# Hybrid decoder layer: the memory branch's output product as seven quarter products, with the weight sums made in DRAM

## The chip, the core and the metric

The kernel runs on one core of one Trainium2 chip. Its time is the device time of one execution, in microseconds; the time before is the median of three runs. The profile is of one further execution. TensorE (PE in the views) multiplies, VectorE (DVE) and ScalarE (ACT) work on tiles in SBUF and PSUM, GpSimd (POOL) and SyncE (SP) mostly issue DMAs.

## What is computed

One decoder layer on 512 tokens of 1024 features. Three token mixers run side by side: a sliding-window attention (branch 0), a stick-breaking attention (branch 1) and a cross-attention to 256 memory rows (branch 2). Each gives 512 features per token, is multiplied by its branch weights (512 x 1024), gated, and summed. Then follow an output product, normalisation with residual, and a SwiGLU feed-forward part.

```python
g = jax.nn.sigmoid(gl.reshape(B, S, N_BRANCH, D))
merged = (g[:, :, 0] * jnp.einsum('bse,ed->bsd', y_swa, w_branch_swa[l])
          + g[:, :, 1] * jnp.einsum('bse,ed->bsd', y_sb, w_branch_sb[l])
          + g[:, :, 2] * jnp.einsum('bse,ed->bsd', y_mem, w_branch_mem[l]))
mix = jnp.einsum('bsd,de->bse', merged, w_out[l])
h = h + rms_norm(mix, ln_mix_post[l])
```

## The kernel before

**Split products.** Float32 factors are split into a high part (rounded, made by ScalarE) and a low part (the rest, made by VectorE). `mm3` makes a product as three TensorE products: high by high, high by low, low by high. So each weight tile of 128x1024 costs a load (SP), a high part (`hi`, ScalarE) and a low part (`lo`, VectorE) before TensorE can use it. `split` and `w_split` do this; all of them are recorded under line 202, so tiles tell them apart.

**The stream.** The work of TensorE up to the output product is a list of units in `dn`: projections, values, memory keys and values, gates, branch products. `Stream.piece` starts a unit by loading weights four units ahead, splitting three ahead, calling the unit's `begin` functions, and then issuing its products. Attention heads are issued in between. This fixes only the program order. The order in which each engine runs its instructions is written out by hand in ORDER, one list of program numbers for each engine, and PLAN gives each tile its buffer.

**The start.** [...] SP and ScalarE's queue load x (eight pieces x[0] to x[7] of 128x512, `xT`) and the first three weight tiles in pieces. Each x[k] is multiplied by its gain and split into `uh` and `ul`; TensorE then runs nine products for each k (three weight tiles by three). It has nothing else to do until all eight pieces are used. POOL first clears eight tiles (`qbl`), and later writes the row of norms to DRAM (`row_x`) and reads it back turned, for the scaling of the values.

**Quarter products.** The gates of all branches and the product of branch 0 are made as seven products of quarters instead of eight. Tokens are cut into two halves and features into two halves; the factors are sums of quarters. For the gates and for branch 0 the sums of weight quarters were made by DMAs that add into the raw weight buffer in place, issued by POOL one after the other as the previous use of the buffer ended (`q_issue`, `seven_issue`). The sums of y are made on VectorE (`seven_sums`, four operations), after ScalarE has copied y in quarters (`seven_raw`), and split by `seven_split`. `seven` issues 12 products for each of p1, p2, p5, p3, p6, p7, p4; `seven_end` copies p1 and p5 aside, joins results, and `seven_out` multiplies by the gate and adds.

**The memory branch and the mix.** The memory branch was made plainly by `branch_t`: two halves of the output, four token tiles each, four chunks of y, three products. After each tile VectorE multiplies by the gate and adds the sum of the others. `merge(0)` turned (transposed on TensorE) the left half of the merged features for all four token tiles, `merge(1)` the right half, each followed by a split; `mix_mm` multiplies the turned tiles by the output weights `wo`, whose 16 tiles are split on ScalarE and VectorE during the gates and branch of the memory. The mix of tiles 0 and 1 was made in two halves, with `merge(1)` between them. Then `mix` normalises a tile of tokens and the feed-forward part begins.

Of the kernel before, what the change touches and what calls it, by code (L numbers as in the profile page):

```python
# [17 lines left out]
P = 128  # L18
# [3 lines left out]
KC = D // P  # L22
# [8 lines left out]
SEVENS = (SWA,)  # L31
# [19 lines left out]
    ),  # L51
    "vector": (
# [32 lines left out]
    ),  # L85
    "scalar": (
# [26 lines left out]
    ),  # L113
    "gpsimd": (
        "5-12 4 2-3 16 0 29 1 14 13 15 30 22 17 27 23 25 24 26 21 20 19 18 28 31-34 36-37 35 38 40 39 41-49 51 50 "
        "52-55 57 56 58-60 63 61-62 64-69 74 70 73 75 71-72 76-99 111-116 107 100-106 108-110"
    ),
    "sync": (
# [1928 lines left out]
```

## Time and profile before

| | us |
|---|---|
| median of 3 runs | 783.73 (783.63 to 783.98) |
| profiled execution | 783.61 |
| its span | 781.8 |
| TensorE busy in it | 773.5 |
| VectorE busy | 614.6 |
| ScalarE busy | 480.7 |
| POOL busy | 92.2 |

The span runs from the first instruction to the last; what lies around it is the difference to the execution's time. Matmuls overlap in the records, so a record is longer than the distance from one start to the next. Times in the views are us from the start of the span. The granted clock of TensorE was 0.999 of full speed.

### The profile page before, as it was taken

To read this page: it belongs to the slowest core of one execution; us is meant where nothing else is said; L and a number is where in the kernel's file an instruction comes from. 1 tells how busy PE (TensorE), PEld (TensorE's weight loads), DVE (VectorE), ACT (ScalarE), POOL (GpSimd) and SP (SyncE) were. 2 spreads that over 40 slices of the span, in tenths; PEclk is the share of its full clock that TensorE was granted. 3 is DMA by queue.
4 is the path that set the end of the run, shared out by engine and by line. 5 is a ranking of instruction groups with operands and counts; after the bars stand their busy time and mean duration, and the time that the engine had idled before them with its cause. 6 is when DMAs were issued, how large, how long until landed. Compare 5 with 4: busy or idle time off the path is not lost.

```text
span 781.8 us, 12301 instructions
## 1 busy us (share of the span) xinstructions
PE 773.5 (99%) x4626; PEld 678.8 (87%) x4626; DVE 614.6 (79%) x982; ACT 480.7 (61%) x862; POOL 92.2 (12%) x121
## 2 busy tenths in 40 slices
PE   9999999999999999999999999999999999999996
PEld 6899888788888888877888899999999999888885
DVE  6994787677887757999874599977777879997686
ACT  7662677786586658676653486445555456866662
POOL 3100400000112121020012001000000000215000
PEclk9999999999999999999999999999999999999999
DMA  8443923245459697589998138977767653959602
GB/s 302 141 130 122 319 84 109 81 135 149 94 122 199 164 193 168 98 225 205 338 334 169 22 82 232 252 190 189 186 178 189 176 160 99 232 113 246 123 2 107
DMA packets 44652, 130.18 MB, mean 167 GB/s; under 512 B 5296, under 2 KB 6880, under 8 KB 44592
## 3 DMA queue, kind: packets, MB, share of 16 engines
q1 hardware_dynamic: 30336, 84.68, 32.9%
q0 software_dynamic: 13824, 44.32, 30.1%
q8 instruction: 36, 0.59, 0.3%
q10 hardware_dynamic: 432, 0.39, 0.1%
q14 instruction: 24, 0.20, 0.1%
HBM read 122.55 MB, written 4.72 MB: 163 GB/s over the span
## 4 chain that ended last, share of the span: by engine, by line
PE 97%; DVE 1%; issue 0%; ACT 0%; DVEq 0%
PE p L202 97%; DVE lo L202 0%; DVE gq0p L202 0%; DVE gq2p L202 0%; ACT hi L202 0%; DVE fg L202 0%; DVE wo03l L202 0%; DVEq L2035 0%; DVE wo11l L202 0%; DVE wo02l L202 0%; DVE s L202 0%; DVE wide L202 0%; DVE wo00l L202 0%; ACT sqr L202 0%; DVE wo01l L202 0%
## 5 line engine op out<-in xcount | busy, mean ns | idle before, releaser
L202 DVE TENSOR_TENSOR lo<-raw,hi 128x1024 fp32r<-128x1024 f32 (+4 forms) x138 | 157.9, 1152 | 53.4 <-ACT hi L202 52.8
L202 ACT CAST hi<-raw 128x1024 fp32r<-128x1024 f32 (+4 forms) x138 | 136.3, 997 | 86.5 <-PE p L202 49.5
L202 ACT CAST hi<-wide 128x1024 fp32r<-128x1024 f32 x57 | 59.7, 1052 | 38.8 <-PE p L202 15.6
L202 DVE TENSOR_TENSOR lo<-wide,hi 128x1024 fp32r<-128x1024 f32 x57 | 69.7, 1224 | 17.2 <-ACT hi L202 16.9
L202 PE MATMUL p<-lo,lh 128*128 128x512 f32 x154 | 59.9, 389 | 0.0
L202 PE MATMUL p<-hi,ll 128*128 128x512 f32 x154 | 59.7, 389 | 0.0
L202 PE MATMUL p<-hi,lh 128*128 128x512 f32 x154 | 59.1, 389 | 0.0
L202 PE MATMUL p<-lo,uh 128*128 128x512 f32 (+1 forms) x160 | 57.3, 358 | 0.0
L202 PE MATMUL p<-hi,ul 128*128 128x512 f32 (+1 forms) x160 | 57.2, 358 | 0.0
L202 PE MATMUL p<-hi,uh 128*128 128x512 f32 (+1 forms) x160 | 56.2, 359 | 0.0
L202 PE MATMUL p<-uh,hi 128*128 128x512 f32 x136 | 54.5, 401 | 0.0
L202 PE MATMUL p<-uh,lo 128*128 128x512 f32 x136 | 53.0, 390 | 0.0
L202 PE MATMUL p<-ul,hi 128*128 128x512 f32 x136 | 53.0, 391 | 0.0
L202 POOL DMA_DIRECT2D wide<-in_w_gu x21 | 18.1, 877 | 185.7 <-DMA wide<-in_w_gu 150.9
L202 PEld LDWEIGHTS p<-lo,lh 128*128 128x128 f32 x154 | 28.9, 188 | 6.0
L202 PEld LDWEIGHTS p<-hi,ll 128*128 128x128 f32 x154 | 28.9, 188 | 6.0
L202 PEld LDWEIGHTS p<-hi,lh 128*128 128x128 f32 x154 | 28.9, 188 | 5.9
L202 PEld LDWEIGHTS p<-hi,uh 128*128 128x128 f32 x160 | 30.0, 188 | 4.3 <-DVE wide L202 0.3
L202 PEld LDWEIGHTS p<-lo,uh 128*128 128x128 f32 x160 | 30.0, 188 | 4.0 <-DVE lo L202 0.4
L202 PEld LDWEIGHTS p<-hi,ul 128*128 128x128 f32 x160 | 30.0, 188 | 3.7
L202 POOL DMA_DIRECT2D raw<-in_w_g x24 | 20.7, 861 | 104.8 <-DVE lo L202 95.4
L202 ACT COPY gp<-p 128x512 f32<-128x512 f32 x33 | 19.3, 586 | 22.0 <-PE p L202 21.4
(687 smaller groups left out, 2405.5 us busy)
## 6 DMA issues: line engine op xcount, KB each, us to landing
wide<-in_w_gu SPq DMA_DIRECT2D x31, 512.0 KB, 5.3
raw<-in_w_gu SPq DMA_DIRECT2D x26, 512.0 KB, 5.2
raw<-in_w_g POOLq DMA_DIRECT2D x24, 512.0 KB, 7.4
wide<-in_w_gu POOLq DMA_DIRECT2D x21, 512.0 KB, 8.4
raw<-in_w_g SPq DMA_DIRECT2D x18, 512.0 KB, 5.0
raw<-in_w_p SPq DMA_DIRECT2D x14, 512.0 KB, 3.7
raw<-in_w_brt SPq DMA_DIRECT2D x11, 512.0 KB, 4.8
bp<-in_w_dn SPq DMA_DIRECT2D x22, 256.0 KB, 6.4
```

Of the source, the lines that this page charges most:

```text
L202: ins = f(*args, **kw)
```

## The change

Branch 2 joins branch 0 in the seven quarter products. It takes the sums of weight quarters, for both branches, out of the raw buffers: for each of the two branches `w_sum` makes p5, p6, p4 and p7's weights in DRAM, by a copy and an adding DMA each, both on POOL, begun at units 17 to 24 in program order. p6's copy reads p5's sum, p4's reads p6's. The quarters are then loaded like any other weight. y of the memory branch is copied in quarters, and its four sums are made once the last pair of heads is out. `merge(i)` now turns both halves of the features for two token tiles: `merge(0)` tiles 0 and 1, `merge(1)` tiles 2 and 3. The mix of tile 0 and of tile 1 is each made in one go, and `merge(1)` follows them. All orders and buffer plans are written anew; the first entries of POOL's are shown.

```diff
-SEVENS = (SWA,)
+SEVENS = (SWA, MEM,)
+SUM_FROM = 17
...
     "gpsimd": (
-        "5-12 4 2-3 16 0 29 1 14 13 15 30 22 17 27 23 25 24 26 21 20 19 18 28 31-34 36-37 35 38 40 39 41-49 51 50 "
+        "5-12 31 33 4 39 41 32 34 40 42 16 2-3 35 0 43 29 36 1 44 37 45 38 14 13 15 30 46 17 22 27 21 20 19 18 23 "
...
-    def seven_issue(b, p):
-        j, h = QSRC[p]
-        src = a["w_brt"][:, b, h, 2 * j : 2 * j + 2].rearrange("p k n -> p (k n)")
-        if p in ("p1", "p2", "p3"):
-            sw[(b, p)] = w_load(src, 1024)
-            return
-        old = {"p5": "p1", "p6": "p5", "p4": "p6", "p7": "p3"}[p]
-        t = sw[(b, p)] = sw.pop((b, old))
-        nc.gpsimd.dma_start(t[:, :], src, accum_op=ALU.add)
+    wsum = {}
+    WSUM = dict(p5=((0, 0), (0, 1)), p6=("p5", (1, 1)), p4=("p6", (1, 0)), p7=((1, 1), (0, 1)))
+
+    def w_quarter(b, j, h):
+        return a["w_brt"][:, b, h, 2 * j : 2 * j + 2].rearrange("p k n -> p (k n)")
+
+    def w_sum(b, p):
+
+        old, more = WSUM[p]
+        t = wsum[(b, p)] = drm.tile([P, 1024], F32, name=f"ws{b}{p}")
+        nc.gpsimd.dma_start(t[:, :], wsum[(b, old)][:, :] if isinstance(old, str) else w_quarter(b, *old))
+        nc.gpsimd.dma_start(t[:, :], w_quarter(b, *more), accum_op=ALU.add)
...
+        return lambda: w_load(wsum[(b, p)][:, :] if p in WSUM else w_quarter(b, *QSRC[p]), 1024)
...
-    def merge(h):
+    def merge(i):
+
 
         for c in range(4):
-            pt = (dps if (h, c) in ((1, 0), (1, 1)) else aps)(f"mg{h}{c}")
-            for t in range(NT):
-                nc.tensor.transpose(
-                    pt[:, t * P : (t + 1) * P], gate_t[(MEM, t, h)][:, c * P : (c + 1) * P], ident[:, :]
-                )
...
+            pt = aps(f"mg{i}{c}")
+            for k in range(2):
+                h, o = divmod(2 * c + k, 4)
+                for t in range(2):
+                    nc.tensor.transpose(
+                        pt[:, (2 * k + t) * P : (2 * k + t + 1) * P],
+                        gate_t[(MEM, 2 * i + t, h)][:, o * P : (o + 1) * P],
+                        ident[:, :],
+                    )
...
-        for g, p in enumerate(QUART):
-            if p not in ("p1", "p2", "p3"):
-                dn.units[g0 + g - 5]["begin"].append(lambda p=p: seven_issue(b, p))
-        dn.units[g0 - 4]["begin"].append(lambda: seven_sums(b))
...
+        for i, p in enumerate(("p5", "p7", "p6", "p4")):
+            dn.units[SUM_FROM + 4 * SEVENS.index(b) + i]["begin"].append(lambda p=p: w_sum(b, p))
+        if b == SWA:
+            dn.units[g0 - 4]["begin"].append(lambda: seven_sums(b))
...
         if b in SEVENS:
             seven_raw(b, c, ps)
+            if b != SWA and c == 3:
+                seven_sums(b)
...
-    mix_mm(0, 0, 4)
+    merge(0)
+    mix_mm(0, 0, KC)
+    tmp[0] = mix(0)
+    mix_mm(1, 0, KC)
     merge(1)
-    mix_mm(1, 0, 4)
-    mix_mm(0, 4, KC)
-    tmp[0] = mix(0)
-    mix_mm(1, 4, KC)
```

POOL's numbers 31 to 46 in the new order are the 16 DMAs of `w_sum`, in pairs of copy and adding DMA: branch 0's p5, p7, p6, p4 (31 to 38), then branch 2's (39 to 46). 0 is the write of `row_x`, 1 its read-back, 5 to 12 the eight clears. In the new TensorE order the products of one x[k] with the three first weight tiles begin with the three high by high ones. In the new VectorE order the low parts of the output weights 05, 06, 07 and 14 to 17, and the last joins, multiplications and additions of token tiles 2 and 3, stand behind the low parts of `merge(0)`.

More of the change, by code (lines that the diff above doesn't have):

```diff
@@ L36 @@
     "tensor": (
[14 rows of a table removed]
[17 rows of a table added]
     ),
     "vector": (
[32 rows of a table removed]
[33 rows of a table added]
     ),
     "scalar": (
[26 rows of a table removed]
[28 rows of a table added]
     ),
     "gpsimd": (
-        "5-12 4 2-3 16 0 29 1 14 13 15 30 22 17 27 23 25 24 26 21 20 19 18 28 31-34 36-37 35 38 40 39 41-49 51 50 "
-        "52-55 57 56 58-60 63 61-62 64-69 74 70 73 75 71-72 76-99 111-116 107 100-106 108-110"
+        "5-12 31 33 4 39 41 32 34 40 42 16 2-3 35 0 43 29 36 1 44 37 45 38 14 13 15 30 46 17 22 27 21 20 19 18 23 "
+        "28 25 24 26 47-48 50 49 53 52 51 54-55 57 56 58-65 67 66 68-81 86 82 85 87 83-84 88-111 123-128 119 "
+        "112-118 120-122"
     ),
     "sync": (
-        "0-14 16-18 15 19-27 32 28-31 33-34 36-38 35 39-52 57 60 53-56 63-64 58-59 61-62 65-90 93-94 91-92 97-98 "
-        "95-96 99-211"
+        "0-14 16-18 15 19-27 32 28-31 33-34 36-38 35 39-52 57 60 53-56 63-64 58-59 61-62 65-94 97-98 95-96 101-102 "
+        "99-100 105-106 103-104 109 107-108 110-218"
     ),
@@ L124 @@
     "raw": (
-        "0 3 2 1 0 3 2 1 0 3 2 1 0 3 2 1 0 3 2 1 0 3 2 1 0 3 2 1 0 3 2 1 0 3 2 1 0 3 2 3 2 3 2 1 0 1 0 1 0 3 2 0 3 "
-        "1 3 1 3 1 2 3"
+        "0 3 2 1 0 3 2 1 0 3 2 1 0 3 2 1 0 3 2 1 0 3 2 1 0 3 2 1 0 3 2 1 0 3 2 1 0 3 2 3 2 3 2 1 0 1 0 1 0 3 1 2 0 "
+        "3 1 2 0 3 0 3 0 3 1 2 0 3 1"
     ),
@@ L129 @@
         "0 3 2 1 0 3 2 1 0 3 2 1 0 3 2 1 0 3 2 1 0 3 2 1 0 3 2 1 0 3 2 1 0 3 2 1 0 3 2 1 0 3 2 1 0 3 2 1 0 3 2 1 0 "
-        "3 2 1 0 3 2 1 0 3 2 1 0 3 2 1 0 3 2 1 0 3 2 1 0 3 2 1 0 3 2 1 0 3 2 1"
+        "3 2 1 0 3 2 1 0 3 2 1 0 3 2 1 0 3 2 1 0 3 2 1 0 3 2 1 0 3 2 1 0 3 2 1 0 3 2"
     ),
@@ L133 @@
         "0 3 2 1 0 3 2 1 0 3 2 1 0 3 2 1 0 3 2 1 0 3 2 1 0 3 2 1 0 3 2 1 0 3 2 1 0 3 2 1 0 3 2 1 0 3 2 1 0 3 2 1 0 "
-        "3 2 1 0 3 2 1 0 3 2 1 0 3 2 1 0 3 2 1 0 3 2 1 0 3 2 1 0 3 2 1 0 3 2 1"
+        "3 2 1 0 3 2 1 0 3 2 1 0 3 2 1 0 3 2 1 0 3 2 1 0 3 2 1 0 3 2 1 0 3 2 1 0 3 2"
     ),
     "p": (
[5 rows of a table removed]
[5 rows of a table added]
     ),
@@ L166 @@
         "0 14 15 13 1 12 2 4 3 5 7 6 8 10 9 11 15 0 14 12 13 1 3 2 4 5 6 7 8 9 10 11 0 1 15 13 14 12 2 4 3 5 6 11 "
-        "7 10 8 9 15 13 0 14 12 5 1 4 2 3 7 10 6 8 9 14 11 13 15 0 1 4 12 2 3 5 7 10 6 11 8 9 13 0 15 14 1 12 4 2 "
+        "7 10 8 9 15 13 0 14 12 5 2 4 1 3 7 10 6 8 9 14 11 13 15 0 2 4 12 1 3 5 7 10 6 11 8 9 13 0 15 14 2 12 4 1 "
         "6 11 3 8"
@@ L170 @@
     "spare": (
-        "0 3 1 2"
+        "1 4 2 3 4 0 1 3"
     ),
     "fraw": (
-        "0 8 7 6 5 1 2 4 3 0 8 7 6 5 0 1 3 4 6 7 2 0 8 5 1 4 7 3 6 2 8 1 0 5 4 3 2 7 6 8 0 4 1 5 3 7 8 2 6 0 1 3 4 "
-        "5 7 2 0 8 6 1 4 7 3"
+        "0 8 7 6 5 1 2 4 3 0 8 7 6 5 0 1 3 4 6 2 7 0 8 5 1 4 2 3 6 7 8 1 0 5 4 3 7 2 6 8 0 4 1 5 3 2 8 7 6 0 1 3 4 "
+        "5 2 7 0 8 6 1 4 2 3"
     ),
@@ L673, in mem_vals @@
         return gen
-    merged = [None] * 8
+    merged = {}
     QUART = ("p1", "p2", "p5", "p3", "p6", "p7", "p4")
@@ L827, in tile_kernel @@
     yq, ysum = {}, {}
-    def seven_issue(b, p):
-        j, h = QSRC[p]
-        src = a["w_brt"][:, b, h, 2 * j : 2 * j + 2].rearrange("p k n -> p (k n)")
-        if p in ("p1", "p2", "p3"):
-            sw[(b, p)] = w_load(src, 1024)
-            return
-        old = {"p5": "p1", "p6": "p5", "p4": "p6", "p7": "p3"}[p]
-        t = sw[(b, p)] = sw.pop((b, old))
-        nc.gpsimd.dma_start(t[:, :], src, accum_op=ALU.add)
-    def seven_got(b, p):
-        def got():
-            if p in ("p1", "p2", "p3"):
-                seven_issue(b, p)
-            return sw[(b, p)]
-        return got
+    wsum = {}
[7 more added lines that the diff above has]
+        nc.gpsimd.dma_start(t[:, :], w_quarter(b, *more), accum_op=ALU.add)
+    def seven_got(b, p):
+        return lambda: w_load(wsum[(b, p)][:, :] if p in WSUM else w_quarter(b, *QSRC[p]), 1024)
     def seven_raw(b, c, ps):
@@ L873, in seven_out @@
     def seven_out(b, t, h, x):
+        if b == SB:
+            acc_t[(t, h)] = x
+            return
         g = gate_t[(b, t, h)]
@@ L888, in seven_end @@
         if p in ("p1", "p5"):
-            t = spare(f"s{p}{b}{i}")
+            t = (ck if b == SB else spare)(f"s{p}{b}{i}")
             with tc.high_priority():
@@ L893, in seven_end @@
         elif p == "p2":
+            if b == SB:
+                t = ck(f"bs{i}")
+                nc.scalar.copy(t[:, :], ps[:, :])
+                ps = t
             seven_out(b, i, 0, ps)
@@ L908, in seven_end @@
             seven_out(b, 2 + i, 0, join(t, ps, t, ALU.add))
-            if b == MEM and i == 1:
-                merge(0)
     def seven(b, p):
@@ L957, in branch_t @@
         return gen
-    def merge(h):
+    def merge(i):
         for c in range(4):
-            pt = (dps if (h, c) in ((1, 0), (1, 1)) else aps)(f"mg{h}{c}")
-            for t in range(NT):
-                nc.tensor.transpose(
-                    pt[:, t * P : (t + 1) * P], gate_t[(MEM, t, h)][:, c * P : (c + 1) * P], ident[:, :]
-                )
-            mh, ml = ck(f"mgh{h}{c}", F32R), ck(f"mgl{h}{c}", F32R)
-            split(pt[:, :], mh[:, :], ml[:, :])
-            merged[4 * h + c] = (mh, ml)
+            pt = aps(f"mg{i}{c}")
[7 more added lines that the diff above has]
+                    )
+            merged[(i, c)] = ck(f"mgh{i}{c}", F32R), ck(f"mgl{i}{c}", F32R)
+            split(pt[:, :], merged[(i, c)][0][:, :], merged[(i, c)][1][:, :])
     for c in range(8):
@@ L985, in add_sevens @@
             dn.add(seven_got(b, p), 1024, seven(b, p))
-        for g, p in enumerate(QUART):
-            if p not in ("p1", "p2", "p3"):
-                dn.units[g0 + g - 5]["begin"].append(lambda p=p: seven_issue(b, p))
-        dn.units[g0 - 4]["begin"].append(lambda: seven_sums(b))
-        for g, p in ((1, "p5"), (2, "p3"), (3, "p6"), (4, "p7")):
-            dn.units[g0 + g]["begin"].append(lambda p=p: seven_split(b, p))
+        for i, p in enumerate(("p5", "p7", "p6", "p4")):
+            dn.units[SUM_FROM + 4 * SEVENS.index(b) + i]["begin"].append(lambda p=p: w_sum(b, p))
+        if b == SWA:
+            dn.units[g0 - 4]["begin"].append(lambda: seven_sums(b))
+        for g, p in ((2, "p5"), (3, "p3"), (4, "p6"), (5, "p7")):
+            dn.units[g0 + g - (b == SWA)]["begin"].append(lambda p=p: seven_split(b, p))
         dn.mark(f"branch{b}")
@@ L1462, in mix_mm @@
     def mix_mm(t, k0, k1):
-        tok = slice(t * P, (t + 1) * P)
-        if k0 == 0:
+        begun = t in mixed
+        if not begun:
             mixed[t] = [aps(f"mx{t}{h}") for h in range(2)]
-        order = [(h, k) for h in range(2) for k in range(k0, k1)] if k0 == 0 else [(h, k) for k in range(k0, k1) for h in range(2)]
+        order = [(h, k) for h in range(2) for k in range(k0, k1)] if not begun else [(h, k) for k in range(k0, k1) for h in range(2)]
         for h, k in order:
-            x = (merged[k][0][:, tok], merged[k][1][:, tok])
+            x = cols(merged[(t // 2, k // 2)], (k % 2) * 256 + (t % 2) * P, P)
             mm3(mixed[t][h][:, :], x, cols(wo[(h, k)], 0, 512), k == 0, k == KC - 1)
```

196 rows, old and new, of tables (ORDER, PLAN) are left out of this document.

## Prediction, before the result was known

> **What bounds the kernel now.** I read the page first: the span, the busy table, the chain that ended last.
>
> ```profile
> span 781.8 us, 12301 instructions
> PE 773.5 (99%) x4626; PEld 678.8 (87%) x4626; DVE 614.6 (79%) x982; ACT 480.7 (61%) x862; POOL 92.2 (12%) x121
> PE 97%; DVE 1%; issue 0%; ACT 0%; DVEq 0%
> ```
>
> TensorE is busy 99% of the span and is 97% of the chain. So a product less on TensorE is time saved, if nothing else makes TensorE wait. Next the pace of one product, from the timeline of the memory branch: the same factor pair on one token tile and on the next one, 12 products on.
>
> ```profile
> 380.12 0.39 PE L202 MATMUL p<-hi,y21l 128*128 128x512 f32 x1
> ...
> 382.84 0.39 PE L202 MATMUL p<-hi,y21l 128*128 128x512 f32 x1
> ```
>
> A record lasts 0.39 us, but 12 products start within 2.72 us, so one costs 0.227 us. Last the chain in order of time, for where something other than TensorE sets it, and the busy times of that stretch (columns: window, length, then busy us and count of PE, PEld, DVE, ACT, POOL; clock, DMA share, GB/s).
>
> ```profile
> 332.10 16.13 PE p L202 x71
> ...
> 349.35 1.17 DVE lo L202
> ...
> 358.84 1.23 DVE lo L202
> ...
> 360.12 415.43 PE p L202 x2732
> 320.00:340.00 20.00, 19.93 (x96) 15.51 (x95) 19.70 (x36) 12.61 (x28) 2.58 (x3) 1.00 0.64 134
> 340.00:360.00 20.00, 19.55 (x90) 15.62 (x88) 18.43 (x27) 15.21 (x22) 3.44 (x4) 1.00 0.96 232
> 360.00:380.00 20.00, 19.89 (x87) 16.28 (x88) 16.35 (x21) 14.56 (x21) 1.72 (x2) 1.00 0.93 265
> 380.00:400.00 20.00, 20.00 (x98) 16.80 (x97) 17.27 (x28) 10.37 (x18) 1.72 (x2) 1.00 1.00 377
> 400.00:420.00 20.00, 20.00 (x98) 16.76 (x97) 9.26 (x15) 6.49 (x13) 5.18 (x6) 1.00 1.06 255
> ```
>
> From 348 to 360 the chain runs through VectorE, which is busy 71.75 of the 80 us from 320 to 400. This is where the extra vector work of the change falls, so there lies one danger. The other is the start, below.
>
> **The products.** The memory branch had 2 halves x 4 token tiles x 4 chunks x 3 products = 96; seven quarter products of 2 x 2 x 3 make 84. The turns are 32 before and after. The TensorE order is 4560 entries before and 4548 after. So 12 x 0.227 = **-2.72 us**.
>
> **The sums in DRAM, at the start.** The w_sum calls issue 16 DMAs of 512 KB on POOL: for each of two branches four copies from DRAM to DRAM and four accumulating ones. Four accumulating ones go (the old in-place sums). In the new POOL order the first of them (its numbers 31, 33, 39, 41, the copies for p5 and p7 of both branches) stand right behind the eight memsets, so they are issued from about 5.2 us on. That is where loads of x and of the first weights keep the DMA engines full, and TensorE has nothing else to do:
>
> ```profile
> 0.73 4.43 POOL L202 MEMSET qbl<- 64x512 f32 x8 [0.29 <-POOLq L2029]
> 7.05 1.61 SPq L202 DMA_DIRECT2D xT<-in_xT  x3
> xT<-in_xT SPq DMA_DIRECT2D x3, 256.0 KB, 5.5
> 12.60 0.72 ACT L202 ACTIVATE uh<-xT,wide 128x512 fp32r<-128x512 f32 x1
> 13.81 0.74 DVE L202 SCALAR_TENSOR_TENSOR ul<-xT,wide,uh 128x512 fp32r<-128x512 f32 x1
> 15.71 0.39 PE L202 MATMUL p<-uh,hi 128*128 128x512 f32 x1
> 10.00:12.00 2.00, 2.00 (x10) 1.65 (x10) 1.80 (x3) 2.00 (x5) 0.00 (x0) 1.00 1.06 400
> ```
>
> The last three pieces of x are issued at 7.05 to 8.7 and land about 5.5 us later. The first of them is x[5]: its high part begins at 12.60, its low part ends at 13.81 + 0.74 = 14.55, and TensorE uses it from 15.71 (27 products of 0.227 behind the third part, nine for each part). The new TensorE order takes the three high products of a part first, so the low part is due at 15.71 + 3 x 0.227 = 16.39. Slack: 1.84 us. At 400 GB/s and a full share (1.06), a copy of 0.524 MB takes 1.31 us of all engines, four 5.2 us; the trace has no copy from DRAM to DRAM, so this is the price of a load. How late x[5] comes depends on who goes first. The nearest row is a load that SP issued at 81.01 behind two POOL transfers:
>
> ```profile
> raw<-in_w_mk SPq DMA_DIRECT2D x4, 512.0 KB, 3.9
> bscr<-brow POOLq DMA_DIRECT2D x1, 1536.0 KB, 6.9
> rows_v<-wide POOLq DMA_DIRECT2D x1, 1024.0 KB, 11.1
> raw<-in_w_mv SPq DMA_DIRECT2D x1, 512.0 KB, 9.2
> ```
>
> A like load took 3.9 us with little beside it, this one 9.2. With even turns between the queues it would have waited for as much again as its own 1.3 us; it waited 5.3, towards the 6.6 us that the 2.6 MB ahead of it need. That is nearer to "what is issued first goes first". By that order two copies (issued at 5.2 and 6.1) stand ahead of x[5], which comes 2.6 us late, 0.8 us beyond its slack. Bounds: 0, if x keeps its pace (nothing is taken away there, so no gain); 4.7 us, if all four copies get ahead (5.2 - 1.84 = 3.4) and half of the first accumulating DMA too. For that one the page's queue rows serve: 30.1% of 781.8 us for the 44.32 MB of q0, 5.3 us for a MB.
>
> ```profile
> q1 hardware_dynamic: 30336, 84.68, 32.9%
> q0 software_dynamic: 13824, 44.32, 30.1%
> ```
>
> So 2.78 us for 0.524 MB of q0, most of it accumulating, against 1.6 us on q1. I take **+0.8 us**. [...]
>
> POOL's own queue: behind the waiting sums stand row_x and its read-back (28.79 and 30.96 before), moved behind nine and three sums. VectorE needs the read-back first at 62.9, when it scales the values:
>
> ```profile
> 30.96 0.81 POOL L202 DMA_DIRECT2D wide<-row_x  x1
> 62.89 1.93 DVE L202 TENSOR_SCALAR wide<-p,wide 128x320 f32<-128x320 f32 x4 [1.43 <-PE p L202]
> ```
>
> Three waits in a row for landings of at most 11.1 us (the longest above), from 5.2, give 39 for the read-back: cost nothing, with over 20 us of cover. SP's seven further loads at 1.3 us of DMA time each replace four sums on the raw buffers; they lie among loads that are issued ahead, cost nothing, or with that cover gone 1.3 us once.
>
> **The extra vector work.** Removed on VectorE: 8 multiplications, 8 additions. Added: four sums of y, four low parts of them, three low parts of weights (7 loads for 4), 26 joins, multiplications and additions. Net 21 instructions, 18 of 128x512 and 3 of 128x1024. ScalarE gets 8 half copies, 4 high parts, 4 copies, 3 high parts of weights.
>
> ```profile
> L202 DVE TENSOR_TENSOR yq<-yq,yq x4: 685/692/694, 231.0 to 233.2; 128x512 f32<-128x512 f32 x4
> L202 DVE TENSOR_TENSOR gq2p<-p,gq2p 128x512 f32<-128x512 f32 x12 | 8.2, 690 | 4.2 <-PE p L202 3.7
> L202 DVE TENSOR_TENSOR lo<-raw,hi 128x1024 fp32r<-128x1024 f32 x31 | 37.3, 1220 | 6.1 <-ACT hi L202 6.1
> L202 ACT COPY yq<-p x8: 350/374/387, 185.9 to 230.4; 128x256 f32<-128x256 f32 x8
> L202 ACT COPY wide<-p 128x512 f32<-128x512 f32 x4 | 2.5, 614 | 0.0
> L202 ACT CAST hi<-raw 128x1024 fp32r<-128x1024 f32 x30 | 31.0, 1055 | 6.7 <-PE p L202 3.5 <-issue 1.7 <-DMA raw<-in_w_g 1.4
> ```
>
> VectorE: 18 x 0.69 + 3 x 1.22 = 16.1 us. ScalarE: 8 x 0.37 + 8 x 0.61 + 3 x 1.06 = 11.0 us; it has 52.75 of 80 busy, so that is covered. VectorE has 8.25 us free, so not all fits. But the new order puts seven low parts of output weights (4.8 us) and the last ten operations of token tiles 2 and 3 (6.9 us) behind the low parts of the first turned half. Before those stand 71.75 + 16.1 - 4.8 - 6.9 = 76.2 us of work. TensorE reaches the fourth pair of merged chunks 18 products into the mix. The mix began at 399.79:
>
> ```profile
> 399.79 0.39 PE L202 MATMUL p<-wo00h,mgh 128*128 128x512 f32 x1
> ```
>
> So it is wanted at 399.8 - 2.7 + 4.1 = 401.2, 81 us after 320: it fits with 5 us to spare, if VectorE's waits for others don't exceed that. They were 8.25 us before, so the bound below allows for them. What hides the rest is the mix of tiles 0 and 1, 96 x 0.227 = 21.8 us, against 4.8 + 6.9. Gone with the old halves: the left half waited for all four tiles.
>
> The turn itself: the second pair of turns needs the additions that stand behind p7's last join; p4's 12 products (2.7 us) cover a join and two additions (3 x 0.69 = 2.1). The spare 0.6 us is thin. On the other side, the new VectorE order moves weights' low parts in 320-360 ahead of sums that nobody waits for yet, and two TensorE waits could go. What can be gained: the rows' idle time, 0.07 + 0.45 + 0.11, about 0.6 us, and what overlapping records hide, no more than again as much. Bounds -1.3 and +3.3 (8.25 - 5.0, all of VectorE's former waits passed on). I take **0**, nearest to the 0.6.
>
> **Sum.** The profiled execution took 783.61 us (span 781.8 and 1.8 around it): 783.61 - 2.72 + 0.8 + 0 = 781.7. It lies 0.12 below the median of the runs, 783.73, so **781.8**; with 0 to 1.5 us at the start and -0.7 to +0.5 in the middle, 780.3 to 783.0 is this case's own range.
>
> **Rivals.**
> 1. *The sums take the start.* The queues share evenly, all four copies and half a sum come ahead of x[5], and weights for the next product tile queue up too. For it: a full DMA share (the 10 to 12 row), no other work for TensorE, and in the new order TensorE takes high products first, as if low parts were late. Against it: the 9.2 us row. Price 4.7 us, up to 6.5 with a second sum: 783.73 - 2.72 + 4.7 to 6.5 = **785.7 to 787.5**. It makes the kernel slower from the point where x[5] comes more than 1.84 + 4.3 us late.
> 2. *VectorE becomes the bound.* TensorE stops at the turns or at a low part. For it: 90% busy already, 5 us to spare. Against: 11.7 us moved behind the turn. 2 to 3.3 us lost: **783.6 to 784.9**, no change.
> 3. *All goes well:* the start costs nothing and the two waits vanish: 783.73 - 2.72 - 1.3 = **779.7**, from 778.9 to 780.3.
>
> That the change doesn't remove the 12 products I leave out: the orders count them.
>
> **Chances.** A measurement here can tell about 0.2%, 1.57 us: faster is below 782.16, slower above 785.30. Forecast 0.42 (0.34 of it faster, 0.08 the same); rival 1 0.26 (0.02 the same); rival 2 0.20 (the same); rival 3 0.12. Together faster 0.46, same 0.30, slower 0.24. The range 779.4 to 786.4 leaves out some 0.05 of rival 3 and 0.12 of rival 1.
>
> **What would show it.** TensorE's count down by 12. The start: where uh of x[5] begins (12.60 before) and TensorE's first gap; a gap above 3 us is rival 1. From 320 to 400: no DVE pieces in the chain, or short ones; long ones before the first mix product are rival 2. The first mix product should come at 399.8 - 2.7 + 0.8 = 397.9, the feed-forward part unchanged. A loss after 420 would make the whole reading wrong.

## The result, and the profile after

The changed kernel takes **789.34 us** (median; 787.51 to 790.21) against 783.68 us of the kernel before on the same chip (783.55 to 783.98): 1.0069 times, 95% interval 1.005 to 1.0087. It is slower by 5.7 us where 1.9 us less was forecast, and lies beyond the forecast's range of 779.4 to 786.4 us.

The page of its profiled execution (790.21 us) first: the span, TensorE's busy time, the chain that ended last.

```profile
span 788.4 us, 12367 instructions
PE 773.6 (98%) x4614; PEld 678.4 (86%) x4614; DVE 624.5 (79%) x1003; ACT 489.6 (62%) x881; POOL 99.4 (13%) x133
PE 95%; DMA 3%; SPq 0%; DVE 0%; issue 0%; ACT 0%; ACTq 0%; DVEq 0%
```

TensorE has 12 products less (4614 against 4626) and is as long busy as before (773.6 against 773.5). Transfers, which had no share of the chain, now have 3% of it. The chain in order of time says where (start, length, what):

```profile
10.34 21.12 DMA raw<-in_w_p
...
33.88 302.66 PE p L210 x1658
...
336.57 0.06 DVE sy L210
...
336.68 445.37 PE p L210 x2870
```

The load of the fourth weight tile takes 21.12 us from its issue to its landing. From 33.88 to 782.05 the chain is TensorE, but for one short step of VectorE at 336.57: the VectorE pieces that stood in it from 349 to 360 are gone. So the loss lies before 34 us, and something was won in the middle. ScalarE's and TensorE's timelines show the start; the second number is the length, in brackets stands the idle time before, and what ended it.

```profile
21.27 0.72 ACT L210 ACTIVATE uh<-xT,wide 128x512 fp32r<-128x512 f32 x1 [3.60 <-DMA xT<-in_xT]
...
22.04 1.65 PE L210 MATMUL p<-uh,hi 128*128 128x512 f32 x3 [5.73 <-ACT uh L210]
...
24.46 0.72 ACT L210 ACTIVATE uh<-xT,wide 128x512 fp32r<-128x512 f32 x1 [2.47 <-DMA xT<-in_xT]
...
27.68 0.72 ACT L210 ACTIVATE uh<-xT,wide 128x512 fp32r<-128x512 f32 x1 [1.98 <-DMA xT<-in_xT]
...
28.46 0.50 PE L210 MATMUL p<-uh,hi 128*128 128x512 f32 x1
```

The rows of ACT are x[5] to x[7]. x[5] begins at 21.27 in place of 12.60, TensorE stands still for 5.73 us, and x[7] comes so late that the last nine products start at 28.46. In the windows from 20 us (columns as in the prediction: PE first, PEclk behind the five counts, then the DMA share and GB/s) two things more are to be seen.

```profile
20.00:22.00 2.00, 0.00 (x0) 0.00 (x0) 0.00 (x0) 0.72 (x1) 0.00 (x0) 0.50 1.08 254
22.00:24.00 2.00, 1.96 (x5) 1.57 (x6) 0.75 (x1) 0.00 (x0) 0.00 (x0) 0.50 1.07 257
24.00:26.00 2.00, 2.00 (x6) 1.57 (x5) 0.78 (x2) 1.24 (x2) 0.00 (x0) 0.50 1.05 254
26.00:28.00 2.00, 2.00 (x9) 1.60 (x8) 0.57 (x1) 0.32 (x1) 0.00 (x0) 0.82 1.08 257
```

The DMA engines are full and yet move only about 255 GB/s. And the granted clock of TensorE stands at 0.50 from 20 to 26 us, at the end of the wait and behind it: 5 or 6 products fall into 2 us, where it was 11 from 14 to 16 us (row in the last section).

### The profile page after: what moved, and what is told of

Its sections match the earlier page's. It is cut to its first block, busy times and chain, and to the rows that moved or that the text cites. A ratio compares the mean times of both kernels' runs of the same rounds, so it can differ in the third digit from the quotient of the medians.

```text
span 788.4 us, 12367 instructions
## 1 busy us (share of the span) xinstructions
PE 773.6 (98%) x4614; PEld 678.4 (86%) x4614; DVE 624.5 (79%) x1003; ACT 489.6 (62%) x881; POOL 99.4 (13%) x133
## 4 chain that ended last, share of the span: by engine, by line
PE 95%; DMA 3%; SPq 0%; DVE 0%; issue 0%; ACT 0%; ACTq 0%; DVEq 0%
PE p L210 95%; DMA raw<-in_w_p 3%; SPq L210 0%; DVE lo L210 0%; ACT hi L210 0%; ACTq L210 0%; DVE fg L210 0%; DVEq L2051 0%; DVE s L210 0%; ACT sqr L210 0%; DVE sy L210 0%; DVEq L210 0%
## 5 line engine op out<-in xcount | busy, mean ns | idle before, releaser
L210 DVE TENSOR_TENSOR lo<-raw,hi 128x1024 fp32r<-128x1024 f32 (+4 forms) x145 | 166.5, 1156 | 53.4 <-ACT hi L210 52.7
L210 ACT CAST hi<-raw 128x1024 fp32r<-128x1024 f32 (+4 forms) x145 | 143.7, 998 | 96.8 <-PE p L210 48.4
L210 ACT CAST hi<-wide 128x1024 fp32r<-128x1024 f32 x53 | 55.6, 1050 | 45.3 <-PE p L210 22.0
L210 DVE TENSOR_TENSOR lo<-wide,hi 128x1024 fp32r<-128x1024 f32 x53 | 64.8, 1225 | 16.7 <-ACT hi L210 16.4
L210 PEld LDWEIGHTS p<-uh,hi 128*128 128x128 f32 x136 | 26.4, 195 | 13.7 <-ACT uh L210 7.0
```

The lines of the kernel that those rows point to most:

```text
L210: ins = f(*args, **kw)
```

## Experiments

Each time stands beside that of the kernel before on the same chip (783.88 us for the first four runs, 784.22 for the next four, 783.80 for the last three). In brackets stand the ratio to it and its 95% interval. "Loss" is the difference to before, plus the 3.93 us that the run with all sums late gained: what the start costs.

### The sums late

```diff
-5-12 31 33 4 39 41 32 34 40 42 16 2-3 35 0 43 29 36 1 44 37 45 38 14 13 15 30 46 17 22 ... 24 26 47-48
+5-12 4 16 2-3 0 29 1 14 13 15 30 17 22 ... 24 26 31 33 39 41 32 34 40 42 35 43 36 44 37 45 38 46-48
```

> The changed kernel with nothing moved but the sixteen transfers that make the sums (eight copies, eight accumulating ones): they stand in POOL's queue behind the last load of the bias, at about 106 us, and no longer at 5 us. Theory 1 (the sums take the DMA engines from the token blocks at the start, and nothing else of the change costs time): TensorE's first gap of 5.7 us is gone, x[5]'s high part starts at about 12.6 us as before the change, and the time is 789.3 - 10.9 + at most 1 = 778 to 780 us, faster than both kernels. Theory 2 (the extra work of VectorE and ScalarE, or the sums' traffic wherever it stands, costs the time, and the gap at the start is only where it shows first): 786 us or more.

**779.95 us**, 0.9947 times before (0.9935 to 0.9960), 3.93 us faster. ScalarE's row of x[5] and x[6] in its timeline, then its chain in order of time:

```profile
14.11 1.33 ACT L210 ACTIVATE uh<-xT,wide 128x512 fp32r<-128x512 f32 x2
```

```profile
1.35 325.20 PE p L210 x1744
...
326.58 0.06 DVE sy L210
...
326.69 445.28 PE p L210 x2870
```

TensorE runs from 1.35 to 771.97 us but for one step of VectorE. x[5] starts at 14.11 here, not at 12.6 as expected, but ScalarE did not wait for it (no idle time stands before it), and no product waits for it either. Theory 1 holds: the place of 16 transfers in one queue makes the difference between 0.5% faster and 0.7% slower, and the rest of the change, taken together, gains 3.93 us.

### The first half behind the token blocks

Copies 31, 33, 39, 41 behind POOL's write of the norm row (0), their accumulating transfers behind its read-back (1), the rest late.

> The changed kernel with the first four copies behind the write of the norm row (about 36 us, when all token blocks and the first weight tiles are in), their accumulating transfers behind its read-back, and the other eight at about 106 us. Theory 1 (the sums cost only where they meet the token blocks and the first weights): within 1 us of the run with all sums late, 778 to 781 us. Theory 2' (sums anywhere in the first layer hold up its weight tiles, which a share of 0.3 to 0.4 of the DMA engines doesn't say): 783 us or more, with gaps of TensorE between 36 and 70 us that DMA raw ends.

**779.86 us** (0.9947; 0.9933 to 0.9960). POOL came there sooner than expected, but behind all of x:

```profile
27.88 1.05 POOL L210 DMA_DIRECT2D ws0p<-in_w_brt  x2
28.92 1.02 POOL L210 DMA_DIRECT2D ws2p<-in_w_brt  x2
```

From 28 us on the sums cost nothing; theory 2' falls.

### Four copies, two copies at the start

```diff
-5-12 4 16 2-3 0 ...     (the sums late)
+5-12 31 33 39 41 4 16 2-3 0 ...     (four)
+5-12 31 33 4 16 2-3 0 ...           (two)
```

> As the run with the sums late, but the first four copies (2 MB read and 2 MB written) stay at 5 us behind POOL's memsets; the four accumulating transfers behind them and the other eight stand at about 106 us. Theory 1a (the queues of SP and POOL share the engines, so that SP's token blocks are late by about the copies' own engine time, at most 4 x 1.31 = 5.2 us, less the slack of 1.84 us): 2 to 4 us above the run with all sums late, 781 to 783 us, x[5] at 15 to 17 us. Theory 1b (what is issued first goes first, as the prediction had it): x[5] at 15.2 us, 0.8 us above the run with all sums late, about 780 us. Theory 1c (the copies alone make the whole loss, the accumulating transfers come too late to matter): 786 us or more. If the accumulating transfers are the cause, within 0.5 us of the run with all sums late.

> As the run before this one with only two copies at 5 us. Theory 1a: half the amount, 2.6 us of engine time less 1.84 us of slack, 0.5 to 1 us above the run with all sums late. Theory 1b: within 0.3 us of the run with all sums late. Theory 1c: 3 us or more above it.

Four: **783.68 us** (0.9997; 0.9988 to 1.0005), a loss of 3.73 us. Two: **780.54 us** (0.9959; 0.9946 to 0.9971), a loss of 0.59. The losses are those of theory 1a (2 to 4 us, 0.5 to 1 us). For four copies "what is issued first goes first", with two of them ahead of x[5], gave 0.8, the copies as the whole cause 6 or more. How the queues share is in the DMA rows for 9 to 12 us of the run with four (queue, kind: records, MB, share of 16 engines; q0 is POOL's, q1 carries SP's):

```profile
q0 software_dynamic: 215, 0.81, 71.5%
q1 hardware_dynamic: 214, 0.32, 28.9%
```

215 records against 214: the queues take turns, as many records of one as of the other. But POOL's take 0.715 x 16 x 3 / 215 = 0.160 us, SP's 0.289 x 48 / 214 = 0.065. So equal turns leave SP 29% of the engines, not half. Over all four copies POOL's records took 0.346 x 16 = 5.5 us of each engine (row from 4 to 20 us, two sections on), while SP's loads were on their way. x[5] starts at 18.38, later than the 15 to 17 of theory 1a, and 4.3 us behind the run with sums late:

```profile
18.38 1.38 ACT L210 ACTIVATE uh<-xT,wide 128x512 fp32r<-128x512 f32 x2 [0.60 <-DMA xT<-in_xT]
```

### The same four copies in SP's queue

```diff
-        nc.gpsimd.dma_start(t[:, :], wsum[(b, old)][:, :] if isinstance(old, str) else w_quarter(b, *old))
+        if isinstance(old, str):
+            nc.gpsimd.dma_start(t[:, :], wsum[(b, old)][:, :])
+        else:
+            by_sp.append(nc.sync.engine.dma_start(t[:, :], w_quarter(b, *old)))
...
```

They stand behind the load of the fourth weight tile in SP's order; the other twelve transfers are late.

> The run with four early copies, with these four copies issued by SP behind the fourth weight tile (about 10 to 11.5 us) and no longer by POOL at 5 us; the rest of the sums late as there. The same bytes reach the DMA engines in the same 20 us, but in the queue that carries the token blocks, behind them. Theory 1a (two queues are served in turn, so a second queue takes packets from the token blocks whatever was issued first): x[5] as without early sums, 12.6 to 14.2 us, and 780 to 781 us. Theory of the amount (2 MB more through the engines at the start is what costs): 783 to 784 us as with POOL's queue.

**779.90 us** (0.9951; 0.9938 to 0.9963): no loss. SP issues them from 9.48 us on, and x[5] comes as without them:

```profile
9.48 1.25 SPq L850 DMA_DIRECT2D ws0p<-in_w_brt  x2
10.78 1.36 SPq L850 DMA_DIRECT2D ws2p<-in_w_brt  x2
...
14.34 1.34 ACT L210 ACTIVATE uh<-xT,wide 128x512 fp32r<-128x512 f32 x2
```

So 2 MB more in these 20 us isn't the cost. But this run changed two things, the queue and the place behind x, so by itself it doesn't tell "a second queue pushes in" from "what is issued first goes first". The issues of the changed kernel do (POOL's and SP's timelines):

```profile
5.10 1.22 POOL L210 DMA_DIRECT2D ws0p<-in_w_brt  x2
...
6.63 1.14 POOL L210 DMA_DIRECT2D ws2p<-in_w_brt  x2
12.52 0.87 POOL L210 DMA_DIRECT2D ws0p<-in_w_brt  x1 [4.74 <-DMA ws0p<-in_w_brt]
...
17.79 0.81 POOL L210 DMA_DIRECT2D ws2p<-in_w_brt  x1 [0.65 <-DMA ws2p<-in_w_brt]
```

```profile
7.88 2.42 SPq L210 DMA_DIRECT2D xT<-in_xT  x3
10.34 0.48 SPq L210 DMA_DIRECT2D raw<-in_w_p  x1
```

All four copies were issued ahead of x[5] to x[7]. With four ahead, the prediction's own numbers give 5.2 - 1.84 = 3.4 us by order of issue too, so the loss of 3.73 alone doesn't refute that order. The four accumulating transfers do: they were issued from 12.52 to 17.79, behind the last piece of x and the fourth weight tile, and with them the loss is 9.6 us in place of 3.7. Together with the counts of 215 and 214 this shows what costs here: a second queue, whose records push in between those of the first although they were issued later.

### The copies by halves

Each of the four early copies in two transfers of 512 columns.

> The run with four early copies, each in two transfers of half the columns: the same bytes in POOL's queue at the same place, with packets of 2 KB in place of 4 KB, twice as many. Theory 1a in its sharp form (the queues take turns packet by packet; in the run with four early copies, 9 to 12 us, the two queues moved 215 and 214 packets): each packet of a token block waits for one of half the length, so the loss shrinks to about half, 3.7 us to 1 to 2.2 us: 781 to 782.2 us. If the queues share by time or bytes, or if the amount costs, the loss stays: 783.2 to 784.2 us.

**782.84 us**, a loss of 2.55 us: between the two expectations. It doesn't tell them apart, because it didn't do what it was meant to. From 4 to 20 us, this run and then the run with four copies:

```profile
q0 software_dynamic: 640, 2.10, 35.6%
```

```profile
q0 software_dynamic: 576, 2.10, 34.6%
```

64 records more for the same bytes, not twice as many: the records weren't cut. Nor is the 1.2 us less of loss a gain by the halving: it goes with the granted clock, which is on record for each execution. With four whole copies, the three executions that had a clock of 0.999 took 782.12 to 782.31 us, the eight at 0.996 or 0.997 took 783.48 to 785.24. With halves, six at 0.998 or 0.999 took 781.63 to 782.84, five at 0.995 to 0.997 took 783.39 to 784.49. At like clocks the two hardly differ; more of the halved ones kept theirs. So some 1.5 us of the 3.73 go with the clock behind the wait; why it falls in some executions and not in others stays open.

### Plain copies in place of the accumulating transfers

Four plain copies of the second quarters stand where the changed kernel has 31 33 39 41; 31 33 39 41, which overwrite what these wrote, stand behind them, where it has the accumulating 32 34 40 42. The accumulating ones and the other eight transfers are late.

> The changed kernel's first eight transfers at their places at the start, but the four accumulating ones are plain copies: each sum's tile is first filled with the one quarter, then overwritten by the other, and the accumulating transfer that makes the sum right stands at about 106 us with the remaining eight. The number of packets at the start is the changed kernel's. In the trace of the changed kernel, 18 to 30 us, a packet of POOL's queue took 0.791 x 16 x 12 / 513 = 0.296 us; in the run with four early copies, 9 to 12 us, 0.715 x 16 x 3 / 215 = 0.160 us. Theory 1a with turns by packets (a packet of a token block waits for one whole packet of the other queue): the accumulating part of the loss, 789.3 - 783.7 = 5.6 us, falls by the ratio of these to about 3 us: 786 to 787.5 us. If only the number of packets counts: 789. If accumulating transfers cost by something else, such as their waits on POOL: 783.5 to 785.

**787.00 us** (1.0039; 1.0025 to 1.0053), a loss of 7.1 us, within the 786 to 787.5 of turns by records. This run has as many early transfers as the change (first eight), but shorter records. DMA rows from 12 to 18 us here, then from 18 to 30 us in the changed kernel:

```profile
q0 software_dynamic: 390, 1.43, 63.2%
q1 hardware_dynamic: 515, 0.78, 38.6%
```

```profile
q0 software_dynamic: 513, 1.89, 79.1%
q1 hardware_dynamic: 565, 1.07, 26.7%
```

A record of POOL's takes 0.632 x 96 / 390 = 0.156 us here, and 0.791 x 192 / 513 = 0.296 in the change. The turns are even while both queues have work: 197 and 197 records from 9 to 12 us here, 353 and 354 from 20 to 28 in the change. So the loss grows with the number of POOL's records and with the time of each: 0.6, 3.7, 7.1 and 9.6 us for two copies, four, eight, and four with the accumulating ones behind them. In all of these runs the number of records goes with the bytes; no run told the two apart, since the halves left the records whole.

### The kernel before with early sums

All 16 transfers added to POOL's queue of the kernel before, eight at the start, eight late; nothing reads the sums.

> The kernel before, with the changed kernel's sixteen transfers added to POOL's queue: two copies behind the memsets, two more and the four accumulating ones behind the next instruction, the other eight behind the last load of the bias. Nothing reads the sums; the kernel's own loads of branch weights are left as they are. Theory 1 (the sums at the start are the whole of the loss, and the rest of the change gains what the run with late sums gained): 783.9 + 9.4 = 793.3 us, between 792 and 794.5. If the loss needs another part of the change, such as the longer list of SP's loads or the moved read-back of the norm row: below 790 us.

**794.64 us** (1.0133; 1.0119 to 1.0147): 10.4 us more than before, just above theory 1's range of 792 to 794.5. The early sums do their harm without the rest of the change, so neither SP's longer list nor the moved read-back is needed for it.

### The wait filled

24 products of zeros between the last product of x[4] and the first of x[5].

> The changed kernel as it stands, with 24 products of zeros (24 x 0.227 = 5.4 us at the full clock) added on TensorE between the last product of x[4] and the first of x[5]; they add zeros to a sum under way. They fill the 5.7 us in which TensorE waits for x[5]. Theory C (the clock of 0.50 that the trace shows from 20 to 26 us, after TensorE sat idle, is part of the loss): the products behind run at 0.227 us, the clock stays at 1.00, and the time falls by 2.5 to 3 us, to 786.5 us. Theory L (the loads of x[6], x[7] and the fourth weight tile are the bound in this stretch, and products at half the clock fit between them): the clock stays at 1.00, TensorE waits longer for x[6] and x[7] instead, and the time stays at 788.5 to 789.8 us.

**787.98 us** (1.0057; 1.0044 to 1.0069) against 1.0069 (1.005 to 1.0087) for the change itself: 1 to 2 us less by the medians, but the intervals overlap. That is less than theory C wants, more than theory L. The clock did stay up, and TensorE then waited for x[6] and x[7] instead (0.79 and 0.77 us):

```profile
20.00:22.00 2.00, 2.00 (x10) 0.92 (x8) 0.62 (x1) 0.72 (x1) 0.00 (x0) 1.00 1.07 257
```

```profile
24.61 0.96 PE L211 MATMUL p<-uh,hi 128*128 128x512 f32 x3 [0.79 <-ACT uh L211]
...
27.81 0.50 PE L211 MATMUL p<-uh,hi 128*128 128x512 f32 x1 [0.77 <-ACT uh L211]
```

x[7]'s first product starts at 27.81 in place of 28.46, straight behind its load in both. So the loads bound this stretch, and the slow clock was mostly hidden behind them. That holds for the changed kernel; in the run with four copies, where no later load was waited for, the executions that kept their clock were some 1.5 us shorter (above).

### VectorE's slack in the middle

The run with all sums late, plus 8 or 16 operations on VectorE in a row at 342 us.

```diff
         nc.vector.tensor_tensor(g[:, :], g[:, :], more[:, :], op=ALU.add)
+        if len(nc.vector.seen) - 1 == PAD_AT:
+            for _ in range(PADS):
+                pads.append(nc.vector.engine.tensor_tensor(g[:, :], g[:, :], g[:, :], op=ALU.max))
```

> The run with all sums late, plus eight operations of VectorE on 128x512 f32 (the maximum of a gate tile with itself, which changes nothing) one behind the other at about 342 us: 8 x 0.60 = 4.8 us more of VectorE between 320 and 400 us, where the profile of that run has it busy 79 of 80 us. The prediction's step 4 (the extra vector work fits with 5 us to spare, since much of the busy time is work ahead that may be late): less than 1 us. Rival 2 (VectorE is the bound of the stretch, so that any more is paid): 4 to 4.8 us, 784 to 784.8.

> The same with sixteen, 9.6 us. Step 4: beyond the 5 us to spare, so about 9.6 - 5 = 4.6 us: 783.5 to 785.5. Rival 2: 9 to 9.6 us, 789 to 789.6.

8: **785.92 us** (1.0026; 1.0016 to 1.0036), 6.0 us above the run without them (each by its own before). 16: **792.23 us** (1.0107; 1.0093 to 1.0121), 12.4 us. Both are more than rival 2's full price. The run with 8: timeline of VectorE and TensorE, then the windows of the wait and behind it.

```profile
342.89 5.78 DVE L894 TENSOR_TENSOR gq0p<-gq0p 128x512 f32<-128x512 f32 x8
...
349.67 1.94 PE L213 MATMUL p<-c_ident,mw 128*128 128x128 f32 x8 [3.90 <-DVE mw L213]
```

```profile
346.00:348.00 2.00, 0.00 (x0) 0.00 (x0) 1.90 (x4) 0.90 (x1) 0.00 (x0) 1.00 1.07 229
348.00:350.00 2.00, 0.33 (x2) 0.36 (x3) 2.00 (x4) 0.00 (x0) 0.00 (x0) 0.53 0.26 54
350.00:352.00 2.00, 2.00 (x10) 1.90 (x9) 2.00 (x3) 0.57 (x2) 0.12 (x1) 0.50 0.00 0
...
354.00:356.00 2.00, 2.00 (x8) 1.62 (x7) 2.00 (x5) 0.82 (x3) 0.88 (x1) 0.77 0.94 166
```

The pads took 5.78 us; TensorE stood still for 3.90, so 1.9 us was the slack at this place. Then it ran at half its clock until about 355 us, which makes up the other 2.1 us (6.0 - 3.9): the products from the wait to the first with xsp60h took 10.25 us here (349.67 to 359.92) and 7.68 us in the run without pads (345.81 to 353.49), 2.6 us more in the profiled executions. The slack that step 4 had in mind lies further behind, before the mix. These runs don't test it: the VectorE operation that TensorE waited for stood right behind the pads.

## Why the prediction was wrong

1. **Products, -2.72 us: right as far as the runs show.** The count is down by 12, and the run with sums late is 3.93 us faster; no run took the products alone.
2. **Sums at the start, +0.8 us: this step failed.** Measured: +9.6 us (5.66 + 3.93), twice the upper bound of 4.7. What it had wrong is how much of POOL's traffic comes ahead of the loads. *The order:* it let "what is issued first goes first" decide, charged x[5] with two copies and left the accumulating transfers behind them out (its bound has half of one). The queues take turns (353 and 354 records from 20 to 28 us), all eight transfers ran beside x[5] to x[7] and the fourth weight tile, and x[5] came 8.7 us late, not 2.6. Even by its own rule it had the issues wrong: all four copies, not two, came ahead of x[5] (5.10 to 7.77 against 7.88). *The price* of a transfer in engine time was right: four copies at 1.31 us and four accumulating ones at 2.78 make 16.4 us of each engine, and POOL's queue took 0.358 x 7 + 0.712 x 6 + 0.791 x 12 = 16.3 from 5 to 30 us of the changed kernel (DMA rows from 5 to 12 and 12 to 18; that from 18 to 30 stands above):

```profile
q0 software_dynamic: 224, 0.85, 35.8%
```

```profile
q0 software_dynamic: 392, 1.41, 71.2%
```

   *The row behind the order:* the load of 9.2 us at 81.01 was read as one that stands in line. The DMA rows of the kernel before, from 81 to 85 and from 87 to 89 us, show that for one part of it only:

```profile
q0 software_dynamic: 300, 1.38, 97.3%
```

```profile
q0 software_dynamic: 103, 0.42, 51.9%
q1 hardware_dynamic: 102, 0.41, 50.2%
```

   From 81 to 85 SP's queue moved no record at all: there the load did wait, which turns cannot explain (what held it stays open). Once both queues moved, they took 103 and 102. So the trace of before held a stretch of even turns too, and the prediction didn't look for one. The equal counts don't tell whether a turn is one record of the trace or several.
3. **POOL's and SP's queues, nothing: right.** The read-back of the norm row was issued at 40.08 us (39 was forecast; the order puts eleven sums ahead of it, not twelve), no wait on it shows in the chain, and the run of the kernel before with early sums lost as much without SP's longer list.
4. **Vector work, 0 (-1.3 to +3.3): right in its sum, wrong in its reason.** The run with sums late gained 3.93 - 2.72 = 1.2 us more than the products: the VectorE pieces of 349 to 360 left the chain, as rival 3 had it, which is the likely source. But the "5 us to spare" can't be had anywhere in the stretch: at 342 us the slack was 1.9 us, and pads of 5.78 us cost 6.0. Where the work stands in the order decides, not the free share of a stretch. The marker for it was wrong too: the first mix product came at 401.26 in the change and at 391.17 with sums late, not at 397.9 or 397.1, since the new order of TensorE puts one mix product ahead of the last products of the branch.
5. **Rivals.** Rival 1 named the mechanism (even turns, weights queue up too), had chance 0.26, and gave 785.7 to 787.5; it was short by 1.8 to 3.6 us: it let the four copies and half a sum in, or one sum more, where all four accumulating transfers ran beside the loads. Its marker, a first gap above 3 us, stood at 5.73. Rival 2 didn't occur. Rival 3's 779.7 is what the change gives with its sums elsewhere (779.95).

## What to carry to other kernels

When transfers are put into a second queue while the first one feeds the critical path, ask how many records they bring and how long each takes. In these runs the queues took turns by records (215 and 214, 353 and 354), so the needed queue was left with 29% of the engines beside plain copies (9 to 12 us, four copies) and 27% beside accumulating ones (18 to 30 us, the change), whatever was issued earlier (the stretch from 81 to 85 us of the kernel before is the open exception). So put early work that isn't urgent behind the urgent loads in the same queue, or later; here the first sum is loaded at 306.68 us (SP's timeline of the changed kernel), and the four early sums begun at 28 us cost nothing. And test a reading such as "first come, first served" on a stretch in which both queues really moved records, with the issue times of both.

## What the runs showed of the hardware

- Accumulating transfers from DRAM to DRAM took 0.296 us for a record where plain copies of the same bytes took 0.156 to 0.160; with the engines full, the changed kernel's rate fell from 414 GB/s, before most of them ran, to some 255 (20 to 28 us, above).

```profile
14.00:16.00 2.00, 2.00 (x11) 1.58 (x9) 1.16 (x2) 0.97 (x2) 0.83 (x1) 1.00 1.04 414
```

- After a wait of 5.73 us TensorE's clock stood at 0.50 until about 26.7 us (0.82 on average from 26 to 28), over 4 us behind the first product; after 3.90 us likewise (0.50 from 350 to 352, 0.77 from 354 to 356). After 1.8 us, in the profiled execution with halved copies, it stayed at 1.00:

```profile
16.00:18.00 2.00, 0.50 (x3) 0.07 (x1) 0.73 (x2) 0.76 (x2) 0.00 (x0) 1.00 1.05 396
18.00:20.00 2.00, 1.67 (x7) 1.22 (x8) 0.94 (x2) 1.23 (x3) 0.00 (x0) 1.00 0.98 350
```

  So a wait of some 4 us cost more than itself where TensorE was the bound behind it (2.1 us more in the run with 8 pads), and little where loads were (1 to 2 us by the medians, in the run with the wait filled). From what length of wait on the clock falls, these runs show only roughly. In the run with four copies it stood at 0.50 behind a wait of 3.3 us (row below). With 8 pads the last product ended at 345.77, and the mean of 0.53 from 348 to 350 puts the fall from 1.00 to 0.50 at about 348.1, which is 2.3 us later.

```profile
20.00:22.00 2.00, 2.00 (x6) 1.52 (x6) 1.97 (x4) 1.70 (x4) 0.00 (x0) 0.50 1.02 390
```
